# A hybrid decoder layer on one Trainium2 core: the weight sums of the output product's first pair, made ahead of time and kept in DRAM

## The chip, the cores and the metric

The kernel runs on one core of one Trainium2 chip. The core has TensorE (PE, matmuls), VectorE (DVE), ScalarE (ACT), GpSimd (POOL) and SyncE (SP), each with its own in-order queue of instructions, and 16 DMA engines for transfers. DMAs are issued here by SP and, in a few places, by ACT. The metric is the device time of the whole kernel in microseconds: the median of several runs.

## What is computed

One decoder layer on x of 512 tokens by 2048 features, all in float32:

```python
h = rms_norm(x, norm1_g)
proj = h @ w_in
qa, ka, va, ra, ga, qb, kb, vb = jnp.split(proj, split_points, axis=-1)
log_g = jax.nn.log_sigmoid(ga @ gla_gate_w2 + gla_gate_b) / GLA_GATE_TAU
out_a = gla_mixer(qa, ka, va, ra, log_g, gla_onorm_g)
out_b = dilated_mixer(rms_norm(qb), rms_norm(kb), vb, rel_bias)
mix = jnp.concatenate([out_a, out_b], axis=-1)
x = x + mix @ w_out
h2 = rms_norm(x, norm2_g)
x = x + (jax.nn.silu(h2 @ w_gate) * (h2 @ w_up)) @ w_down
```

out_a is a gated linear attention (4 heads, chunks of 64), out_b a dilated attention (8 heads) whose scores get a bias looked up in rel_bias. The product that the change is about is mix @ w_out, with w_out of 2048 by 2048.

## The kernel before

**Products in pairs.** The large products are computed a pair of column blocks at a time (class Pair). A pair takes two blocks w1, w2 of 512 columns of a weight and the 2048 contraction rows in four groups g of twice 256. For each group it holds four quarters of 256 rows by 512 columns (a and c from w1, b and d from w2; a and b from the group's first rows, c and d from its second), and multiplies by the Strassen-Winograd scheme: seven products P1, P5, P6, P3, P7, P2, P4 in place of eight. Three of them use a single quarter (SINGLE: P1 uses a, P3 uses d, P2 uses c). Four use a difference (SUMS_OF), made in place by VectorE at L256: P5 is b - a, written over a; P6 is d minus that, over a again; P7 is d - b, over b; P4 is c minus P6's sum, over a. The quarters are loaded by SP at L222 into tiles of 512 KB (wpool, 12 buffers).

**Items.** stream() runs over all pairs in order, over the seven products, over the four groups: 28 items a pair. For precision each item's weight is split: ACT casts it to wh (L331), VectorE subtracts to get wl (L335), and TensorE does 12 matmuls of 128x512 (L367), 8 with wh (against the high and low part of the activations) and 4 with wl. wh and wl have two buffers each, so the cast for item k+1 must wait until TensorE is done with item k-1. While item k is multiplied, the program gives the cast of k+1 (first_part), the sum of k+2 (total) and the subtraction for k+1 (second_part).

**The background.** After each item a pair's step function is called. It runs small pieces of other work (the attention chunks, the gates, the operands of the next product) from a list of generators, at a rate given pair by pair (rate, paced). Work tiles of 128x512 come from a pool with tag "r" and four buffers (rpool).

**Order.** The instructions of TensorE, VectorE and ACT are put in an order of their own by a scheduler that lists them for each engine (before the first stream by hand). DMAs are issued in program order on SP. Transfers are counted on eight semaphores, given in turn to those of SP and ACT, and each waits for the one before it on its own.

**The pairs.** After the first pair (qa, ka) come va; then qb and kb, first halves; then vb; then qb and kb, second halves; the gate; then two pairs of w_out (columns 0 to 1023 and 1024 to 2047), the up and gate products, and the down product. The change's words count the first pair as one: pairs two to four are va, qb0/kb0 and vb. A pair can have a before function that is called ahead of its first item. For the third pair (pairs[1]) it only lifts a hold on the order.

**The bias tables.** bias_tables() is a background job begun with the second pair. It makes the dilated attention's bias (bias_d, in DRAM) and at its end, L628, copies it from DRAM to DRAM, repeated for 128 partitions (rep_d, 2.5 MB). The dilated heads load from rep_d at L971.

Other lines that are spoken of: L566 copies a closed sum of a product out of PSUM with a scale (cout, ACT); L1109 stores such results (va, qb, kb, vb) on SP; L886 and its neighbours load q, k and v chunks back; L928 and L933 make the normed attention output oT, and L936 stores it as ong_d. L174 and L175 split activations of the output product in two (AA, AS); L1193 and L1237 load halves of mix from mix_d for them; L1251 to L1255 make their sums (r); L1129 turns the gated part of mix with matmuls into bank, from cr (L1178).

## Time and profile before

| | us |
|---|---|
| median of 3 runs | 1967.47 |
| lowest and highest | 1966.2, 1968.27 |
| the profiled execution, its own time | 1968.84 |
| its span | 1967.1 |

The profile was taken in a fourth execution. Its span runs from the first to the last instruction recorded; its own time also has what lies around it. A page gives busy times of the engines, the span in slices, the DMA queues, the chain of work that ended last, and groups of instructions: line, engine, operation, output <- inputs, count | busy us, mean ns of one | idle time of the engine just before them and what ended it. L is a line of the kernel before. PEld is the load of weights into TensorE, which overlaps its matmuls. A row of a timeline has start, duration, engine, line, operation, tiles, count, and in brackets the idle time ahead of it. ACTq and SPq are the issues of transfers on those queues. A row "A <- B: us, times, longest" sums the waits of A that B ended.

### The profile page before, as it was taken

How to read it: one execution, taken by the hardware profiler on the slowest of the kernel's cores; microseconds unless marked ns; L12 is line 12 of the kernel's file. 1: busy time of each engine (PE TensorE's matmuls, PEld its weight loads, DVE VectorE, ACT ScalarE, POOL GpSimd, SP SyncE). 2: the span in 40 equal slices, each digit the busy share in tenths (PEclk: the TensorE clock that was granted, in tenths of full speed). 3: DMA queues.
4: the chain of work that ended last, by engine and by line, in shares of the span. 5: the costliest groups of instructions: out<-in, count | busy, mean ns of one | idle time of the engine just before them, and what ended most of it. 6: DMA issues, size and time to landing. Idle time of an engine off the chain costs nothing.

```text
span 1967.1 us, 25785 instructions
## 1 busy us (share of the span) xinstructions
PE 1927.6 (98%) x9226; PEld 1670.9 (85%) x9226; DVE 1653.7 (84%) x1850; ACT 1093.8 (56%) x1600; POOL 60.9 (3%) x81
## 2 busy tenths in 40 slices
PE   8999999999999999999999999999999999999998
PEld 7888888888878877888888888888888888888887
DVE  8997787868789889878878878878879989989987
ACT  8554564566766766545545445545446646546443
POOL 0000230010000000000000000000000000000000
PEclk9999999999999999999999999999999999999999
DMA  8447455463766684554554553554555865855662
GB/s 278 141 162 266 119 171 170 134 200 124 221 213 202 215 288 152 177 167 133 178 170 127 179 163 127 176 164 130 172 163 168 299 203 185 310 183 175 236 214 75
DMA packets 237114, 360.45 MB, mean 183 GB/s; under 512 B 18246, under 2 KB 96783, under 8 KB 236984
## 3 DMA queue, kind: packets, MB, share of 16 engines
q1 hardware_dynamic: 236776, 358.72, 57.6%
q8 instruction: 72, 1.18, 0.3%
q14 instruction: 58, 0.48, 0.1%
q10 hardware_dynamic: 208, 0.08, 0.0%
HBM read 296.59 MB, written 64.51 MB: 184 GB/s over the span
## 4 chain that ended last, share of the span: by engine, by line
PE 75%; DVE 8%; DMA 5%; issue 3%; ACT 2%; POOL 0%; SPq 0%; DVEq 0%; ACTq 0%
PE acc L367 71%; DVE wl L335 3%; DVE wa L256 2%; PE bank L1129 1%; DVE AS L175 1%; PE bank L987 1%; DMA q<-in_x 1%; DMA xn_d<-oT 1%; ACT wh L331 1%; DMA q<-y_d 0%; DVE seed L294 0%; PE bank L1019 0%; DVE seed L1334 0%; DMA r<-xn_d 0%; DMA wc<-in_w_down 0%
## 5 line engine op out<-in xcount | busy, mean ns | idle before, releaser
L367 PE MATMUL acc<-wh,AS 128*128 128x512 f32 x3008 | 712.5, 380 | 0.6 <-ACT wh L331 0.5
L367 PEld LDWEIGHTS acc<-wh,AS 128*128 128x128 f32 x3008 | 569.8, 190 | 82.3 <-ACT wh L331 1.8
L331 ACT CAST wh<-wa 128x1024 fp32r<-128x1024 f32 x376 | 394.0, 1048 | 392.4 <-PE acc L367 363.0
L367 PE MATMUL acc<-wh,AA 128*128 128x512 f32 x2256 | 535.0, 380 | 0.0
L335 DVE TENSOR_TENSOR wl<-wa,wh 128x1024 fp32r<-128x1024 f32 x376 | 456.3, 1217 | 69.2 <-ACT wh L331 43.6
L367 PEld LDWEIGHTS acc<-wh,AA 128*128 128x128 f32 x2256 | 427.4, 190 | 61.4 <-ACT wh L331 0.9
L367 PE MATMUL acc<-wl,AS 128*128 128x512 f32 x1504 | 395.3, 385 | 9.7 <-DVE wl L335 9.5
L367 PEld LDWEIGHTS acc<-wl,AS 128*128 128x128 f32 x1504 | 279.4, 189 | 62.0 <-DVE wl L335 21.0
L367 PE MATMUL acc<-wl,AA 128*128 128x512 f32 x1128 | 298.1, 387 | 7.9 <-DVE wl L335 7.7
L367 PEld LDWEIGHTS acc<-wl,AA 128*128 128x128 f32 x1128 | 209.6, 190 | 41.5 <-DVE wl L335 12.4
L331 ACT CAST wh<-wb 128x1024 fp32r<-128x1024 f32 x94 | 98.5, 1049 | 129.7 <-PE acc L367 127.8
L331 ACT CAST wh<-wc 128x1024 fp32r<-128x1024 f32 x94 | 98.4, 1047 | 111.5 <-PE acc L367 101.7
L331 ACT CAST wh<-wd 128x1024 fp32r<-128x1024 f32 x94 | 98.5, 1048 | 105.8 <-PE acc L367 102.3
L256 DVE TENSOR_TENSOR wa<-wc,wa 128x1024 f32<-128x1024 f32 x94 | 114.4, 1221 | 46.2 <-DMA wc<-in_w_gate 25.1
L335 DVE TENSOR_TENSOR wl<-wc,wh 128x1024 fp32r<-128x1024 f32 x94 | 114.5, 1218 | 35.6 <-ACT wh L331 35.6
L335 DVE TENSOR_TENSOR wl<-wd,wh 128x1024 fp32r<-128x1024 f32 x94 | 114.3, 1219 | 34.9 <-ACT wh L331 28.2
L335 DVE TENSOR_TENSOR wl<-wb,wh 128x1024 fp32r<-128x1024 f32 x94 | 113.6, 1216 | 5.5 <-ACT wh L331 5.5
L256 DVE TENSOR_TENSOR wb<-wd,wb 128x1024 f32<-128x1024 f32 x94 | 114.3, 1216 | 1.1 <-DMA wd<-in_w_in 0.6
L256 DVE TENSOR_TENSOR wa<-wb,wa 128x1024 f32<-128x1024 f32 x94 | 113.6, 1218 | 0.8
L256 DVE TENSOR_TENSOR wa<-wd,wa 128x1024 f32<-128x1024 f32 x94 | 112.8, 1215 | 0.1
L298 DVE SCALAR_TENSOR_TENSOR seed<-acc,rs,seed 128x512 f32<-128x512 f32 x96 | 70.4, 745 | 24.9 <-PE acc L367 24.9
L282 ACT ACTIVATE seed<-acc,rs 128x512 f32<-128x512 f32 x96 | 60.6, 681 | 1.4 <-PE acc L367 0.8
(303 smaller groups left out, 1365.1 us busy)
## 6 DMA issues: line engine op xcount, KB each, us to landing
wa<-in_w_gate SPq DMA_DIRECT2D x44, 512.0 KB, 3.9
wb<-in_w_up SPq DMA_DIRECT2D x44, 512.0 KB, 4.3
wd<-in_w_up SPq DMA_DIRECT2D x44, 512.0 KB, 4.3
wc<-in_w_gate SPq DMA_DIRECT2D x44, 512.0 KB, 3.7
wc<-in_w_in SPq DMA_DIRECT2D x28, 512.0 KB, 3.9
wa<-in_w_in SPq DMA_DIRECT2D x24, 512.0 KB, 5.1
wb<-in_w_in SPq DMA_DIRECT2D x24, 512.0 KB, 6.0
wd<-in_w_in SPq DMA_DIRECT2D x24, 512.0 KB, 5.9
```

What stands on the lines that cost most here:

```text
L175: nc.vector.tensor_tensor(a[:, :, 1, :], src, a[:, :, 0, :].bitcast(F32), op=ALU.subtract)
L256: nc.vector.tensor_tensor(src, self.quarter(one, g), src, op=ALU.subtract)
L282: nc.scalar.activation(halves(t), unfolded(src[m]), AF.Copy, scale=self.scale(half, m))
L298: nc.vector.scalar_tensor_tensor(halves(seed[m]), unfolded(src[m]), self.scale(half, m), halves(seed[m]), op0=ALU.mult, op1=ALU.add,)
L331: nc.scalar.copy(high[k], sources[k])
L335: nc.vector.tensor_tensor(low[k], sources.pop(k), high[k].bitcast(F32), op=ALU.subtract)
L367: nc.tensor.matmul(p.dst[prod][m], a[:, jj, hl, m * P : (m + 1) * P], folded(w[:, jj, :]), start=fresh and g == 0 and len(terms) == 2 and ...
L987: nc.tensor.matmul(lp[:, :n], qh[:, b * P : (b + 1) * P], kh[:, :n], start=True, stop=True)
L1129: nc.tensor.transpose(bk[:, jj, m * P : (m + 1) * P], tiles[m][:, f : f + P], ident)
```

## The change

A new generator, weight_sums, makes the four differences of each group of the output product's first pair (w_out, columns 0 to 511 and 512 to 1023) while pairs two to four run, and stores them in 16 DRAM arrays (out_sums). It works in eight blocks of 128 rows (four groups, two halves). Block i starts 12 + 9i items after the second pair's first one; it fetches four pieces of 256 KB by DMAs issued on ACT (a and b at its start, d one item later, c two later) into the "r" tiles, subtracts them on VectorE four to seven items after its start, and stores each difference one item after it is made, again with DMAs issued on ACT. One item's worth is taken after each call of the pair's step function (beside). Every one of these instructions, 64 DMA issues and 32 subtractions of 128x512, is held in its place in program order by tc.keep_in_program_order; the scheduler orders the rest around it.

The output product's first pair is given sums=out_sums: source() then loads the ready difference, 512 KB, into a "w" tile (named ws) instead of computing it, and lets go of the single quarters after their one use. So it makes 28 loads of 512 KB (16 of them sums), in place of 16 loads, and none of its 16 sums at L256. 8 MB of w_out are fetched and 8 MB of sums stored in pairs two to four.

The copy of bias_d into rep_d is taken out of bias_tables (with one yield of that job) and put in the third pair's before function. In SP's order it comes a few loads later than it did. The instructions of GpSimd keep their order; those of the other engines shift.

```diff
--- before.py
+++ after.py
@@ -236,9 +236,10 @@
     class Pair:
 
 
-        def __init__(self, op, rows, w1, w2, final, step, scale=None, before=None):
+        def __init__(self, op, rows, w1, w2, final, step, scale=None, before=None, sums=None):
             self.op, self.rows, self.w1, self.w2 = op, rows, w1, w2
             self.final, self.step, self.scale, self.before = final, step, scale, before
+            self.sums = sums
             self.q, self.dst, self.held = {}, {}, {}
 
         def quarter(self, name, g):
@@ -250,7 +251,14 @@
         def source(self, prod, g):
 
             if prod in SINGLE:
-                return self.quarter(SINGLE[prod], g)
+                t = self.quarter(SINGLE[prod], g)
+                if self.sums:
+                    self.q.pop((SINGLE[prod], g))
+                return t
+            if self.sums:
+                t = wpool.tile([P, 2, 512], F32, name=nm("ws"), tag="w")
+                load(t, self.sums[prod, g])
+                return t
             one, two = SUMS_OF[prod]
             src = self.quarter(two, g)
             nc.vector.tensor_tensor(src, self.quarter(one, g), src, op=ALU.subtract)
@@ -314,6 +322,47 @@
             else:
                 which = {"P3": "P6", "P7": "P5", "P2": "P1"}[prod]
                 self.close(self.held[which], src, *CLOSES[prod])
+
+    def weight_sums(rows, w1, w2, sums):
+
+
+        tt, pinned = nc.vector.tensor_tensor, tc.keep_in_program_order
+        plan = {}
+
+        def at(group, fn):
+            plan.setdefault(group, []).append(fn)
+
+        def block(start, g, j):
+            t = {}
+
+            def fetch(name):
+                r0 = rows[g][0 if name in "ab" else 1] + P * j
+                t[name] = rpool.tile([P, 512], F32, name=nm("r"), tag="r")
+                pinned(nc.scalar.dma_start(t[name], (w1 if name in "ac" else w2)[r0 : r0 + P, :]))
+
+            def less(dst, one, two):
+                pinned(tt(t[dst], t[one], t[two], op=ALU.subtract))
+
+            def put(prod, name):
+                pinned(nc.scalar.dma_start(sums[prod, g][:, j, :], t[name]))
+
+            at(start, lambda: fetch("a"))
+            at(start, lambda: fetch("b"))
+            at(start + 1, lambda: fetch("d"))
+            at(start + 2, lambda: fetch("c"))
+            for i, (dst, one, two, prod) in enumerate(
+                (("a", "b", "a", "P5"), ("b", "d", "b", "P7"), ("d", "d", "a", "P6"),
+                 ("c", "c", "d", "P4"))
+            ):
+                at(start + 4 + i, lambda dst=dst, one=one, two=two: less(dst, one, two))
+                at(start + 5 + i, lambda prod=prod, dst=dst: put(prod, dst))
+
+        for i in range(8):
+            block(12 + 9 * i, i // 2, i % 2)
+        for n in range(max(plan) + 1):
+            for fn in plan.get(n, ()):
+                fn()
+            yield
 
     def stream(pairs):
 
@@ -536,6 +585,15 @@
             except StopIteration:
                 background.pop(0)
 
+    def beside(go, gen):
+
+
+        def both():
+            go()
+            next(gen, None)
+
+        return both
+
     def paced(counts):
         counts = iter(counts)
         return lambda: step(next(counts, 1))
@@ -625,8 +683,9 @@
             nc.vector.tensor_copy(lv, bp[:8, :cn])
             store(bias_d[:, c0 : c0 + cn], lv)
         yield
+
+    def repeat_bias():
         load(rep_d, bass.AP(tensor=bias_d.tensor, offset=0, ap=[[NB, 8], [0, P], [1, NB]]))
-        yield
 
     ss1 = const([P, 4, 4], "ss1")
     rs1 = const([P, 4], "rs1")
@@ -1297,16 +1356,23 @@
     def pair(*args, **kw):
         pairs.append(Pair(*args, **kw))
 
-    pair(opx, rows_in, col(1536), col(1024), final_proj("va1", "va0"), rate((22, 1), (6, 0.6)),
+    ocol = lambda c: w_out[:, c : c + 512]
+    rows_mix = [(1024 + 256 * g, 256 * order[g]) for g in range(4)]
+    out_sums = {
+        (prod, g): dram([P, 2, 512], f"{prod}_{g}_d") for prod in SUMS_OF for g in range(4)
+    }
+    early_sums = weight_sums(rows_mix, ocol(0), ocol(512), out_sums)
+    pair(opx, rows_in, col(1536), col(1024), final_proj("va1", "va0"),
+         beside(rate((22, 1), (6, 0.6)), early_sums),
          row_scale, before=lambda: background.extend([gates(), bias_tables()]))
     flow = rate((90, 0.41))
-    pair(opx, rows_in, col(3088), col(4112), final_proj("qb0", "kb0"), flow, row_scale)
-    pair(opx, rows_in, col(5648), col(5136), final_proj("vb1", "vb0"), flow, row_scale)
+    flowing = beside(flow, early_sums)
+    pair(opx, rows_in, col(3088), col(4112), final_proj("qb0", "kb0"), flowing, row_scale)
+    pair(opx, rows_in, col(5648), col(5136), final_proj("vb1", "vb0"), flowing, row_scale)
     pair(opx, rows_in, col(3600), col(4624), final_proj("qb1", "kb1"), flow, row_scale)
     pair(opx, rows_in, col(2048), col(2560), final_gate, rate((5, 0.6), (23, 1.05)), row_scale)
 
 
-    rows_mix = [(1024 + 256 * g, 256 * order[g]) for g in range(4)]
     x1_d = [dram([P, D], f"x1_d{t}") for t in range(4)]
     xn_d = [dram([P, 2, 512], f"xn_d{b}") for b in range(8)]
     ss2 = const([P, 4, 4], "ss2")
@@ -1417,7 +1483,6 @@
         turn()
         yield
 
-    ocol = lambda c: w_out[:, c : c + 512]
     def output_scales():
         tmp2 = const([P, 4], "tmp2")
         nc.vector.tensor_tensor(tmp2, ss2[:, :, 2], ss2[:, :, 3], op=ALU.add)
@@ -1430,7 +1495,7 @@
     opn = Operand(4)
     tops = [xn_d[2], xn_d[3], xn_d[6], xn_d[7]]
     bots = [xn_d[0], xn_d[1], xn_d[4], xn_d[5]]
-    pair(opm, rows_mix, ocol(0), ocol(512), final_out(0), paced([1] * 28))
+    pair(opm, rows_mix, ocol(0), ocol(512), final_out(0), paced([1] * 28), sums=out_sums)
     pair(opm, rows_mix, ocol(1024), ocol(1536), final_out(1), rate((28, 1.2)))
 
 
@@ -1568,7 +1633,7 @@
     behind = ExitStack()
     for engine in ("act", "dve", "pe"):
         behind.enter_context(tc.issue_after(recent[engine]))
-    pairs[1].before = behind.close
+    pairs[1].before = lambda: (behind.close(), repeat_bias())
     stream(pairs)
     drain()
```

## The prediction

> **What bounds the kernel now.** I read the busy shares first, then the chain's cost groups, and then the one stretch that the change wants to shorten, the output product's first pair.
>
> ```profile
> span 1967.1 us, 25785 instructions
> PE 1927.6 (98%) x9226; PEld 1670.9 (85%) x9226; DVE 1653.7 (84%) x1850; ACT 1093.8 (56%) x1600; POOL 60.9 (3%) x81
> L256 DVE TENSOR_TENSOR wa<-wb,wa 128x1024 f32<-128x1024 f32 x94 | 113.6, 1218 | 0.8
> L335 DVE TENSOR_TENSOR wl<-wa,wh 128x1024 fp32r<-128x1024 f32 x376 | 456.3, 1217 | 69.2 <-ACT wh L331 43.6
> ```
>
> TensorE is busy 98% of the span. All that any change to other engines can recover is where TensorE stands still. So the question is how much it stands still in the output product's first pair, and how much new standing still the early work makes. The L256 row prices one weight sum over a 512 KB quarter at 1.22 us of VectorE.
>
> The next fence has TensorE's order of time at both ends of that pair.
>
> ```profile
> 560.93 1.89 PE L367 MATMUL acc<-wh,AA 128*128 128x512 f32 x8
> ...
> 565.85 1.13 PE L367 MATMUL acc<-wl,AA 128*128 128x512 f32 x4 [0.43 <-DVE wl L335]
> ...
> 570.11 1.13 PE L367 MATMUL acc<-wl,AA 128*128 128x512 f32 x4 [1.40 <-DVE wl L335]
> 573.05 0.44 PE L1129 MATMUL bank<-mats,cr 128*128 128x128 f32 x2 [1.81 <-DVE cr L1178]
> ...
> 574.84 3.02 PE L367 MATMUL acc<-wh,AA 128*128 128x512 f32 x8
> ...
> 578.57 1.89 PE L367 MATMUL acc<-wh,AS 128*128 128x512 f32 x8
> ...
> 642.91 1.89 PE L367 MATMUL acc<-wh,AA 128*128 128x512 f32 x8
> ...
> 645.50 1.89 PE L367 MATMUL acc<-wh,AA 128*128 128x512 f32 x8
> ```
>
> An item (8 matmuls with wh, 4 with wl) takes 645.50 - 642.91 = 2.59 us when nothing holds TensorE. P1's four items run from 560.93 to 578.57, 17.6 us where 4 x 2.59 = 10.4 and 1.7 of turning (573.05 to 574.84) would do. The other 24 run from 578.57 to 645.50, 66.9 us where 24 x 2.59 = 62.2 would do: 4.8 us lost. Where, the windows say (columns: PE, PEld, DVE, ACT, POOL busy with counts, granted clock, DMA share, GB/s):
>
> ```profile
> 560.90:578.60 17.70, 13.89 (x58) 11.05 (x58) 17.38 (x22) 11.71 (x19) 0.00 (x0) 0.90 0.67 218
> 578.60:603.00 24.40, 21.25 (x93) 16.72 (x92) 23.49 (x29) 14.16 (x20) 0.00 (x0) 1.00 0.25 75
> 603.00:625.00 22.00, 22.00 (x104) 19.29 (x103) 22.00 (x27) 15.87 (x24) 0.00 (x0) 1.00 0.69 223
> ```
>
> From 603 us on TensorE is full, so the whole 4.8 us falls in 578.6 to 603, where VectorE is full and TensorE is not.
>
> **What the change takes away.** Sixteen L256 sums leave this pair. VectorE's order of time in the bound stretch, and at the start:
>
> ```profile
> 562.17 1.23 DVE L256 TENSOR_TENSOR wa<-wb,wa 128x1024 f32<-128x1024 f32 x1
> 563.43 1.23 DVE L256 TENSOR_TENSOR wb<-wd,wb 128x1024 f32<-128x1024 f32 x1
> ...
> 570.57 1.22 DVE L256 TENSOR_TENSOR wa<-wb,wa 128x1024 f32<-128x1024 f32 x1
> ...
> 580.11 1.22 DVE L256 TENSOR_TENSOR wa<-wb,wa 128x1024 f32<-128x1024 f32 x1
> 581.24 0.68 DVE L175 TENSOR_TENSOR AS<-r,AS 128x512 fp32r<-128x512 f32 x1
> 581.85 1.22 DVE L335 TENSOR_TENSOR wl<-wa,wh 128x1024 fp32r<-128x1024 f32 x1
> 582.98 0.68 DVE L1251 TENSOR_TENSOR r<-PT,r 128x512 f32<-128x512 f32 x1
> 583.58 1.22 DVE L256 TENSOR_TENSOR wa<-wb,wa 128x1024 f32<-128x1024 f32 x1
> ```
>
> One round of sum, AS, wl and r takes 583.58 - 580.11 = 3.47 us. Without the sum it is 583.58 - 581.24 = 2.34 us, below the item's 2.59. VectorE stops setting the pace there and the 4.8 us come back whole; that is my value for this part, and its lower bound is about 4, if AS waits once for its cast.
>
> At the start, two sums (2.4 us) stand ahead of the wl that TensorE misses at 565.85, and the one at 570.57 ahead of cr. But AA and AS there also hang on a load of mix_d, so only part comes forward. The waits give the ends: nothing, or 0.43 + 1.40 + 1.81 = 3.6 us. I take 2.0, since the 0.43 and some 0.9 of the 1.40 are the sums' and the later wait on cr shrinks by about 0.7. Gain 4.8 + 2.0 = 6.8, between 4 and 8.4.
>
> The matmul row at 574.84 took 3.02 us for what takes 1.89, right after TensorE's idle stretch, and the granted clock of its window is below 1. "TensorE: Matmul & The Clock Gate" of the Trainium skill (Part 1) says that the array's clock is cut after about 3.4 us of idleness; by that rule a shorter gap could also save this 1.1 us. It stays out of the sum.
>
> The pair's transfers grow: 16 loads of ready sums and 12 of single quarters take the place of 16, all of 512 KB, 14 MB for 8 MB. Over 84.6 us this adds 6 x 1.05 / 84.6 = 74 GB/s; the windows above show 218, 75 and 223 GB/s, with DMA shares of 0.67 and less. In SP's order these loads stand far ahead of their use. I cost them at nothing; without the cover a late quarter costs one landing, some 5 us.
>
> **What it adds in pairs two to four.** Eight blocks, each 4 fetches and 4 puts of 256 KB issued by ACT and 4 subtractions of 128x512. Rows of this size:
>
> ```profile
> 1.21 0.47 ACTq L584 DMA_DIRECT2D mats<-in_mats  x1
> ...
> L869 DVE TENSOR_TENSOR T<-k,oT 128x512 f32<-128x512 f32 x4 | 2.8, 689 | 4.2 <-ACT oT L862 4.2
> ...
> 120.00:360.00 240.00, 237.19 (x1164) 203.49 (x1164) 186.38 (x219) 124.73 (x220) 36.54 (x43) 1.00 0.58 183
> 320.00:360.00 40.00, 40.00 (x195) 35.25 (x194) 26.82 (x34) 18.25 (x27) 1.77 (x4) 1.00 0.86 269
> ...
> PE acc L367 <- DVE wl L335: 2.8, 5, 0.9
> ```
>
> The blocks lie within about 133 to 360 us. VectorE gets 32 x 0.69 = 22 us and has 240 - 186.4 = 53.6 us free in the first window; ACT gets 64 x 0.47 = 30 us of issuing and has 115 us free. TensorE loses only 2.8 us to wl between 108 and 400 us (the last row, a sum of waits). By amount everything is covered. A single stolen slot is covered by the two wh and wl buffers: the cast has almost 2.4 us of slack per item. So a subtraction costs something only where it meets a full VectorE. For all 32 I take 0.5 us; the ends are 0 and 0.69 x 8 = 5.5, one late wl per block.
>
> What amounts do not show is **who is queued behind whom**. An ACT issue that has to wait, for a subtraction or for an earlier DMA on its completion lane (the program gives SP's and ACT's transfers eight semaphores in turn, and each waits for the one before it on its own), holds the casts behind it; and SP waits for lanes that ACT's transfers hold, or for the four r buffers. In the new order the sharpest place is the boundary of pairs two and three:
>
> ```profile
> 178.50 1.05 ACT L331 CAST wh<-wa 128x1024 fp32r<-128x1024 f32 x1 [3.63 <-PE acc L367]
> ...
> 183.47 1.26 ACT L566 ACTIVATE cout<-acc,rs 128x512 f32<-128x512 f32 x2 [0.24 <-PE acc L367]
> ...
> 197.69 1.05 ACT L331 CAST wh<-wa 128x1024 fp32r<-128x1024 f32 x1 [0.58 <-DVE wl L335]
> ```
>
> ```profile
> 172.82 1.70 SPq L222 DMA_DIRECT2D wb<-in_w_in  x2
> ...
> 183.48 1.89 PE L367 MATMUL acc<-wh,AA 128*128 128x512 f32 x8
> ...
> 202.97 1.89 PE L367 MATMUL acc<-wh,AS 128*128 128x512 f32 x8
> ...
> SPq L1109 <- ACT cout L566: 5.8, 1, 5.8
> ...
> wb<-in_w_in SPq DMA_DIRECT2D x24, 512.0 KB, 6.0
> ```
>
> The cast of pair three's first item ran at 178.50, 5 us before its use at 183.48. It now stands behind the two cout copies, which need the end of P4. With some attention matmuls moved behind P4, P4 ends near 181.9 and cout near 183.0; the cast ends near 184.1, so TensorE waits 0.6 us, or up to 1.5 if less of that filler is there. I take 1.0.
>
> Second, SP's loads of wb for P5 went out at 172.82; now they stand behind the cout stores, on which SP already waited 5.8 us, behind the ong_d stores, and behind v<-va, which waits for a fetch that ACT issues only after a cast near 191. I put the third wb at about 196.5. With 6.0 us to land, 1.22 for the sum and 1.05 for the cast, wh is ready near 204.8, where the same wh was used at 202.97 (cast at 197.69), now some 1 us later: 0.8 us of waiting, between 0 and 2.5. The other boundaries have nothing so tight in the order, but the same kind of queue; for them and ACT's lane waits I take 0.7, between 0 and 4.
>
> The copy of the bias tables moves by a few places of SP's order:
>
> ```profile
> L628 SPq DMA_DIRECT2D rep_d<-bias_d x1: 718/718/718, 141.2 to 141.2; - x1
> ...
> L971 SPq DMA_DIRECT2D T<-rep_d x4: 338/418/454, 327.2 to 497.9; - x4
> ```
>
> Its first reader is at 327, so that the copy itself costs nothing. It shares a lane with one fetch of block two, near 170, which is after its landing; without that margin ACT would stand still behind it, which is in the 4 us above.
>
> "DMA: Bandwidth & Descriptors" of the Trainium skill (Issuing engines are not separate DMA queues) speaks against the choice of ACT's queue: transfers issued from several engines share the same 16 DMA engines, and only issuing time is saved. By it the 16.8 MB of fetches and puts compete with the pairs' own loads, worst where the 320 to 360 row already has a share of 0.86; no row here shows ACT and SP transfers competing at that point.
>
> **Sum.** -6.8 + 0.5 + 1.0 + 0.8 + 0.7 = -3.8 us. Against the profiled execution, 1968.84 us, this is 1965.0; that execution lies 1.4 us above the median 1967.47 of the runs shown, so on the median the forecast is **1963.7 us**. With the gain between 4 and 8.4 and losses between 0.6 and 6, the case's own range is 1959.7 to 1969.5.
>
> **Rivals.**
>
> *ACT becomes the new wait (slower).* ACT is in order; a put that waits on a lane or a fetch holds the next cast. The nearest row is where ACT waits for a store today:
>
> ```profile
> ACT oT L928 <- DMA ong_d<-oT: 1.9, 2, 1.2
> ```
>
> At 1.2 us twice per block (once at a fetch, once at a put) beyond what the cast's slack covers, eight blocks cost 19 us; minus the 6.8 this is +12, or 1980. At once per block it is 9.6 - 6.8 = +2.8, 1970. It decides against the change from 0.85 us per block on. For it: 64 issues, each with a wait on its lane's predecessor, and SP has a history of waiting on late producers. Against it: most predecessors landed tens of microseconds before, and the slack is 2.4 us per item. I take 1975 for this case, chance 0.26.
>
> *The output product is not freed (about the same).* If mix_d's load and the chain to cr hold the start whatever VectorE does, and the casts of AS hold the middle, 3 us come back, and 3 are lost: 1967.5. For it: AA waits for mix_d. Against it: the 3.47 us round is plainly VectorE's own. Chance 0.18.
>
> *Full relief.* Everything that P1 loses and the clock's dip come back: 17.64 - 10.4 - 1.7 = 5.5 with the 4.8, minus a loss of 1: -9.3, or 1958. The early work then costs nothing but the boundary. Chance 0.14.
>
> **How the numbers follow.** My forecast has 0.42. A measurement of this kernel can tell 0.2% from no change, about 3.9 us, so faster begins below 1963.5. The forecast's case gives 0.24 to faster and 0.18 to same; full relief 0.14 to faster; the unfreed product 0.17 to same and 0.01 to slower; ACT's case 0.25 to slower and 0.01 to same. Faster 0.38, same 0.36, slower 0.26. The range for 8 in 10 goes from 1957, where full relief ends, to 1976, which holds half of ACT's case.
>
> **What would show each step.** In the changed profile: the 578 to 603 stretch at 2.59 us per item with no L256 group on wa<-wb between 560 and 620; the waits of TensorE on wl there below 1 us together (right), or the same 3.5 us rounds (wrong). TensorE's wait at the boundary near 184 and in P5 near 204; idle time of TensorE from 120 to 360, now 240 - 237.2 = 2.8 us, at about 6. In ACT's waits between 130 and 360, a DMA as releaser with more than 10 us in total and the same idleness on TensorE would mean that the first rival holds. The forecast is wrong if TensorE's added idle time before 360 exceeds what 560 to 646 gives back.

## The result, and the profile after

The change makes the kernel 0.2% slower: 1971.68 us median of 14 runs (1966.85 to 1979.36) against 1967.71 us of 14 runs of the kernel before, ratio 1.0021 with a 95% interval of 1.0011 to 1.003. The forecast was 1963.7 us. Runs of the new kernel also scatter about three times as widely in this comparison (12.5 us against 3.7). Lines named from here on are those of the changed kernel where its profile is shown: L380 is the cast to wh (L331 before), L384 the subtraction to wl (L335), L416 the matmul (L367), L264 the sum (L256). P_d stands for the stored sums, so P_d<-r is an early put and r<-in_w_out an early fetch.

First the page of the kernel after, busy times and queues (q10 is the queue of ACT's transfers):

```profile
span 1970.7 us, 25922 instructions
PE 1929.7 (98%) x9226; PEld 1673.4 (85%) x9226; DVE 1654.2 (84%) x1866; ACT 1094.0 (56%) x1600; POOL 53.6 (3%) x81
...
q1 hardware_dynamic: 237992, 365.01, 57.8%
q10 hardware_dynamic: 9424, 16.86, 2.5%
...
L416 PE MATMUL acc<-wh,AS 128*128 128x512 f32 x3008 | 714.3, 381 | 5.8 <-ACT wh L380 5.8
```

VectorE's total is the same (the sums moved, they did not go), 16.86 MB of traffic are new, and a wait of TensorE is there that was not: 5.8 us on casts. To place it, the table below lines up the two profiles by item. TensorE's matmuls were counted off in twelves; for each item it gives how much later its first matmul starts than in the profile of before, less the difference at item 0. Items 0 to 27 are the pair va, 28 to 55 qb0/kb0, 56 to 83 vb, 84 to 139 the next two, 140 to 167 the output product's first pair, 168 to 195 its second. All later tables have the same columns.

| start of item | 28 | 36 | 48 | 84 | 140 | 168 | 224 |
|---|---|---|---|---|---|---|---|
| after, us late | 0.8 | 8.0 | 11.9 | 14.3 | 13.3 | 7.7 | 3.3 |

So 14.3 us are lost by item 84, where the early work ends; 5.6 come back in the output product's first pair (13.3 to 7.7), and another 5.4 in places that the change does not touch (14.3 to 13.3, and 7.7 to 3.3). Two steps stand out in the loss, 32 to 36 and 44 to 48.

TensorE's waits in the kernel after, from 100 to 400 us, and its order of time at the two steps:

```profile
PE acc L416 <- DVE wl L384: 6.6, 7, 2.0
PE acc L416 <- ACT wh L380: 5.8, 3, 4.1
```

```profile
209.41 3.62 PE L416 MATMUL acc<-wh,AS 128*128 128x512 f32 x8 [4.05 <-ACT wh L380]
...
249.91 1.75 PE L416 MATMUL acc<-wl,AS 128*128 128x512 f32 x4 [1.98 <-DVE wl L384]
251.45 3.01 PE L416 MATMUL acc<-wh,AS 128*128 128x512 f32 x8
```

Against 2.8 us before, TensorE waits 12.4 us. Each step also pays twice: after its wait, eight matmuls take 3.62 and 3.01 us in place of 1.89. The first wait leads back through ACT and VectorE to a load. ACT's order of time, then VectorE's:

```profile
208.31 1.04 ACT L380 CAST wh<-wa 128x1024 fp32r<-128x1024 f32 x1 [6.70 <-DVE wa L264]
```

```profile
206.97 2.48 DVE L264 TENSOR_TENSOR wa<-wb,wa 128x1024 f32<-128x1024 f32 x2 [5.95 <-DMA wb<-in_w_in]
...
244.14 1.23 DVE L264 TENSOR_TENSOR wa<-wc,wa 128x1024 f32<-128x1024 f32 x1 [2.12 <-DMA wc<-in_w_in]
```

VectorE waits 6 us for the third wb of the third pair, and ahead of the second step for wc: weight loads, which SP issues. SP's order of time in the kernel after, and what SP itself waited for from 190 to 200 us:

```profile
173.03 1.63 SPq L222 DMA_DIRECT2D wa<-in_w_in  x3
182.72 0.92 SPq L1168 DMA_DIRECT2D va<-cout  x2
...
187.98 0.80 SPq L995 DMA_DIRECT2D ong_d<-oT  x2
188.83 1.00 SPq L222 DMA_DIRECT2D wb<-in_w_in  x2
...
193.54 0.89 SPq L995 DMA_DIRECT2D ong_d<-oT  x2
194.48 3.14 SPq L897 DMA_DIRECT2D T<-ls_d  x3
...
199.01 0.51 SPq L904 DMA_DIRECT2D v<-va  x1
199.56 0.98 SPq L222 DMA_DIRECT2D wb<-in_w_in  x2
200.84 4.08 SPq L222 DMA_DIRECT2D wd<-in_w_in  x4
```

```profile
SPq L995 <- DVE oT L992: 2.8, 1, 2.8
SPq L897 <- DMA P_d<-r: 1.7, 2, 1.2
```

The third wb goes out at 199.56 where it went out at 172.82 before. It stands behind stores that wait for the attention, and behind the loads T<-ls_d, which wait until early puts have landed, since they share a semaphore with them. Then it shares the DMA engines with the fourth wb, four wd and the block's own transfers. A windows row of the kernel before and one of the kernel after, the columns as in the prediction:

```profile
190.00:210.00 20.00, 19.80 (x95) 16.73 (x94) 19.14 (x19) 10.92 (x14) 6.26 (x3) 1.00 0.21 62
```

```profile
190.00:210.00 20.00, 14.92 (x68) 11.84 (x67) 11.04 (x12) 6.83 (x12) 0.99 (x3) 0.98 0.96 309
```

Before, these 20 us were a lull for the DMA engines (share 0.21, 62 GB/s), since the pair's weights were already there. After, they are full (0.96, 309 GB/s). Not all of that is the early work's, as the run with the copy moved alone shows below.

In the output product's first pair the change does what it says. Its waits of TensorE, 574 to 660 us, and a window where the sums stood before:

```profile
PE acc L416 <- DVE wl L384: 1.6, 1, 1.6
PE acc L416 <- ACT wh L380: 0.8, 1, 0.8
PE bank L1188 <- DVE cr L1237: 0.8, 1, 0.8
```

```profile
590.10:610.80 20.70, 20.70 (x97) 18.15 (x96) 20.39 (x27) 17.13 (x27) 0.00 (x0) 1.00 0.99 347
```

P5 and P6 now run without a gap: TensorE is busy 20.70 of 20.70 us, 8 items at 2.59. The row shows full DMA engines too, 0.99 and 347 GB/s, with the ready sums among the loads.

### The profile page after: what moved, and what is told of

Its sections match the earlier page's. It is cut to its first block, busy times and chain, and to the rows that moved or that the text cites. A ratio compares the mean times of both kernels' runs of the same rounds, so it can differ in the third digit from the quotient of the medians.

```text
span 1970.7 us, 25922 instructions
## 1 busy us (share of the span) xinstructions
PE 1929.7 (98%) x9226; PEld 1673.4 (85%) x9226; DVE 1654.2 (84%) x1866; ACT 1094.0 (56%) x1600; POOL 53.6 (3%) x81
## 3 DMA queue, kind: packets, MB, share of 16 engines
q10 hardware_dynamic: 9424, 16.86, 2.5%
## 4 chain that ended last, share of the span: by engine, by line
PE 57%; DVE 5%; DMA 3%; issue 2%; ACT 1%; SPq 0%; DVEq 0%; ACTq 0%
PE acc L416 56%; DVE wl L384 2%; PE bank L1188 1%; DVE wa L264 1%; DVE AS L175 1%; DMA wc<-in_w_down 1%; DMA wb<-in_w_down 0%; DMA xn_d<-oT 0%; DVE seed L1400 0%; DMA r<-xn_d 0%; DVE seed L302 0%; DMA wd<-in_w_down 0%; DMA xn_d<-PT 0%; DVE AA L175 0%; DMA k<-y_d 0%
## 5 line engine op out<-in xcount | busy, mean ns | idle before, releaser
L416 PE MATMUL acc<-wh,AS 128*128 128x512 f32 x3008 | 714.3, 381 | 5.8 <-ACT wh L380 5.8
L416 PEld LDWEIGHTS acc<-wh,AS 128*128 128x128 f32 x3008 | 570.8, 190 | 88.5 <-ACT wh L380 7.8
L380 ACT CAST wh<-wa 128x1024 fp32r<-128x1024 f32 x364 | 381.4, 1049 | 385.8 <-PE acc L416 346.8
L416 PE MATMUL acc<-wh,AA 128*128 128x512 f32 x2256 | 534.3, 380 | 1.5 <-ACT wh L380 1.4
L384 DVE TENSOR_TENSOR wl<-wa,wh 128x1024 fp32r<-128x1024 f32 x364 | 442.1, 1218 | 63.9 <-ACT wh L380 39.3
L416 PEld LDWEIGHTS acc<-wh,AA 128*128 128x128 f32 x2256 | 427.1, 190 | 62.5 <-ACT wh L380 2.4
L416 PE MATMUL acc<-wl,AS 128*128 128x512 f32 x1504 | 395.7, 386 | 9.0 <-DVE wl L384 8.8
L416 PEld LDWEIGHTS acc<-wl,AS 128*128 128x128 f32 x1504 | 280.0, 189 | 60.5 <-DVE wl L384 19.7
L416 PE MATMUL acc<-wl,AA 128*128 128x512 f32 x1128 | 297.6, 386 | 7.6 <-DVE wl L384 7.5
L416 PEld LDWEIGHTS acc<-wl,AA 128*128 128x128 f32 x1128 | 209.5, 189 | 41.4 <-DVE wl L384 11.9
L380 ACT CAST wh<-wb 128x1024 fp32r<-128x1024 f32 x90 | 94.2, 1048 | 127.5 <-PE acc L416 115.9
L380 ACT CAST wh<-wc 128x1024 fp32r<-128x1024 f32 x94 | 98.4, 1047 | 118.7 <-PE acc L416 107.1
L380 ACT CAST wh<-wd 128x1024 fp32r<-128x1024 f32 x94 | 98.4, 1048 | 102.7 <-PE acc L416 99.8
L384 DVE TENSOR_TENSOR wl<-wc,wh 128x1024 fp32r<-128x1024 f32 x94 | 114.6, 1220 | 40.7 <-ACT wh L380 40.6
L264 DVE TENSOR_TENSOR wa<-wc,wa 128x1024 f32<-128x1024 f32 x90 | 109.8, 1222 | 46.1 <-DMA wc<-in_w_gate 23.9
L384 DVE TENSOR_TENSOR wl<-wd,wh 128x1024 fp32r<-128x1024 f32 x94 | 114.4, 1220 | 33.7 <-ACT wh L380 26.8
L264 DVE TENSOR_TENSOR wa<-wb,wa 128x1024 f32<-128x1024 f32 x90 | 108.6, 1219 | 7.1 <-DMA wb<-in_w_in 6.4
L384 DVE TENSOR_TENSOR wl<-wb,wh 128x1024 fp32r<-128x1024 f32 x90 | 108.8, 1217 | 3.3 <-ACT wh L380 3.3
L264 DVE TENSOR_TENSOR wb<-wd,wb 128x1024 f32<-128x1024 f32 x90 | 109.4, 1217 | 0.4
L264 DVE TENSOR_TENSOR wa<-wd,wa 128x1024 f32<-128x1024 f32 x90 | 108.1, 1216 | 0.1
```

Of the source, the lines that this page charges most:

```text
L264: nc.vector.tensor_tensor(src, self.quarter(one, g), src, op=ALU.subtract)
L380: nc.scalar.copy(high[k], sources[k])
L384: nc.vector.tensor_tensor(low[k], sources.pop(k), high[k].bitcast(F32), op=ALU.subtract)
L416: nc.tensor.matmul(p.dst[prod][m], a[:, jj, hl, m * P : (m + 1) * P], folded(w[:, jj, :]), start=fresh and g == 0 and len(terms) == 2 and ...
```

## The experiments

Each kernel was run beside the kernel before on the same chip. The lateness figures of the expectations are without the correction at item 0; the tables have it (0.1 to 1.6 us per profile). They come from one profile each, and the runs of most of these kernels scatter by some microseconds, so differences below about 2 us are not read. Some profiled executions lie well off their kernel's median (without subtractions 3.6 us above it, GpSimd's queue 2.4 below, the kernel before 1.4 above), so the medians are read beside them. The ratio is the recorded one and not the quotient of the two medians.

**The two halves by themselves.** First the early work alone:

```diff
-    pair(opm, rows_mix, ocol(0), ocol(512), final_out(0), paced([1] * 28), sums=out_sums)
+    pair(opm, rows_mix, ocol(0), ocol(512), final_out(0), paced([1] * 28))
```

> The early sums are made and stored as in the change, but the output product's first pair makes its own sums again, as before; nothing is left out of the result. In the changed profile TensorE is 14.4 us late by the start of the fifth pair (item 84: 373.44 us against 358.99) and then wins about 10 us back. Theory Q (queues: the loss comes from the early work alone, by the order and the waits of SP's and ACT's transfers): item 84 is again 12 to 16 us late and nothing is won back, so the median is 12 to 16 us above before, near 1982. Rival U (the lost time belongs to the two parts together, or is noise of one profile): item 84 less than 7 us late, median below 1975.

Then the use alone, in which the ready sums are plain quarters of w_out and no early work is done:

```diff
-        (prod, g): dram([P, 2, 512], f"{prod}_{g}_d") for prod in SUMS_OF for g in range(4)
+        (prod, g): ocol(0)[256 * g : 256 * g + 256, :].rearrange("(j p) n -> p j n", p=P)
+        for prod in SUMS_OF for g in range(4)
...
-    early_sums = weight_sums(rows_mix, ocol(0), ocol(512), out_sums)
+    early_sums = iter(())
...
-    pairs[1].before = lambda: (behind.close(), repeat_bias())
+    pairs[1].before = behind.close
```

> The output product's first pair loads its sums ready made, but they are never made: in their place it loads plain quarters of w_out, so the output's values differ; no early work, and the copy of the bias tables stands where it stood. This is the gain alone. By the prediction's term 6.8 us are gained (4 to 8.4), median near 1961; by the changed profile, where lateness falls from 13.44 at item 140 to 3.44 at item 224, it is up to 10 us, median near 1957.5. Rival (the gain seen there was only slack that a late start gives back): 3 us or less, median 1964.5 or more.

And the copy's move alone, on the kernel before:

```diff
-        load(rep_d, bass.AP(tensor=bias_d.tensor, offset=0, ap=[[NB, 8], [0, P], [1, NB]]))
-        yield
+    def repeat_bias():
+        load(rep_d, bass.AP(tensor=bias_d.tensor, offset=0, ap=[[NB, 8], [0, P], [1, NB]]))
...
-    pairs[1].before = behind.close
+    pairs[1].before = lambda: (behind.close(), repeat_bias())
```

> The kernel before with one edit: the copy of the bias tables is taken out of its job and put in the third pair's before function. By the prediction's term it costs nothing: within 1.5 us of before. Rival: the copy's place changes the order of the background's loads at the boundary near 180 us by itself, 3 us or more slower, and item 36 is late.

| kernel | median us | ratio to before (95%) | 28 | 36 | 48 | 84 | 140 | 168 | 224 |
|---|---|---|---|---|---|---|---|---|---|
| early work alone | 1977.43 | 1.006 (1.0044 to 1.0076) | 0.7 | 7.8 | 12.0 | 13.9 | 13.0 | 12.6 | 9.7 |
| use alone | 1961.04 | 0.9975 (0.9958 to 0.9991) | 0.0 | -0.4 | -0.4 | -0.4 | -0.7 | -4.7 | -6.3 |
| copy moved alone | 1967.86 | 1.0005 (0.9995 to 1.0014) | -0.2 | 1.0 | 3.0 | 3.1 | 2.2 | 1.3 | -1.6 |

The two halves add up: 1977.43 and 1961.04 are +10.6 and -5.8 against the 1966.83 of before beside them, together +4.8, and the change measured +4.0. The gain was forecast at 6.8 and is 5.8. Of the gain, items 144 to 152 (P5 and P6) bring 4.7 in the use alone and 4.8 in the change, as forecast; P1 brings 0.6 and 1.9 of the 2.0 forecast. The loss is 13.9 us where it is made and 9.7 by item 224. The expectation had the median at 12 to 16 above before, and it came to 10.6. It is not shown why some 4 us come back: the use alone, which is not late, also wins 1.6 from item 168 to 224.

The copy's move costs 3.1 us by item 84 in its profile, though over the whole kernel its interval includes no change (+1.0 us), so the price of nothing held for the total. SP's order of time in that kernel, with no early work in it, then VectorE's:

```profile
172.62 1.52 SPq L222 DMA_DIRECT2D wa<-in_w_in  x3
182.31 0.92 SPq L1110 DMA_DIRECT2D va<-cout  x2
...
195.28 0.98 SPq L222 DMA_DIRECT2D wb<-in_w_in  x2
```

```profile
202.15 2.49 DVE L256 TENSOR_TENSOR wa<-wb,wa 128x1024 f32<-128x1024 f32 x2 [4.17 <-DMA wb<-in_w_in]
```

This is the order of the change already: wa behind the va stores, the third wb at 195.28 (172.82 before). Moving one 2.5 MB copy by a few places has put the third pair's loads behind stores that wait for the attention's results. By itself that costs 1.0 us at item 36. VectorE has the wb 6.9 us after its issue here, against 7.4 in the change, and the DMA engines are as full without any early work: share 0.96, 318 GB/s from 195 to 207 us, where the change has 0.97 and 317. So the landing under a full load comes with the order alone; what the early work adds is that the load goes out 4.3 us later, 199.56 for 195.28.

**Which cause in the early work.** Four runs undo one thing each. The transfers on GpSimd's queue:

```diff
-                pinned(nc.scalar.dma_start(t[name], (w1 if name in "ac" else w2)[r0 : r0 + P, :]))
+                pinned(nc.gpsimd.dma_start(t[name], (w1 if name in "ac" else w2)[r0 : r0 + P, :]))
...
-                pinned(nc.scalar.dma_start(sums[prod, g][:, j, :], t[name]))
+                pinned(nc.gpsimd.dma_start(sums[prod, g][:, j, :], t[name]))
```

> The whole change, with its 64 fetches and puts issued by GpSimd's queue in place of ACT's, held in order there; no other edit. Theory Q says that ACT no longer stands behind lanes and SP no longer waits for the puts' semaphores: item 84 at most 5 us late (14.4 in the change) and the median 1960 to 1965, below before. Rival B (bandwidth: 16.8 MB compete with the weight loads whichever queue issues them): item 84 again 10 us or more late, median 1968 to 1974. Rival D (VectorE's 32 subtractions are what costs): the same as B.

The copy back where it stood (the inverse of the diff of the copy's move):

> The whole change, but with the copy of the bias tables left at the end of its job, where it stood before; SP's third and fourth wb of the third pair then stand ahead of the cout and ong_d stores again, as in the kernel before. Theory O (order: most of the early loss comes from the copy's new place, which moves the third pair's weight loads behind those stores): item 36 at most 3 us late (8.17 in the change, 1.72 with the copy's move alone), item 84 at most 7, and with the gain the median near 1962 to 1965. Rival T (traffic: the 16.8 MB and 64 issues themselves make those loads late, wherever they stand): item 36 at least 6 us late and item 84 at least 11, median 1969 to 1972.

No subtractions:

```diff
-                at(start + 4 + i, lambda dst=dst, one=one, two=two: less(dst, one, two))
+                pass
```

> The whole change, copy moved too, but without its 32 subtractions on VectorE: the pieces fetched are stored as they are, so that the output's values differ; all 64 transfers stay. Theories O and T: VectorE's amount is not the cost, so item 36 is 6 to 8 us late and item 84 9 to 13 (14.4 in the change), median 1967 to 1970. Rival D (the subtractions, through a full VectorE or as what ACT's puts wait for): item 84 at most 6 us late, median 1963 or less.

Nothing held in program order:

```diff
-        tt, pinned = nc.vector.tensor_tensor, tc.keep_in_program_order
+        tt, pinned = nc.vector.tensor_tensor, lambda i: i
```

> The whole change without holding the 64 issues and 32 subtractions in program order; the scheduler places them. Theory O: in SP's order the third pair's wb loads stand ahead of the cout stores here although the copy is moved, so item 36 is at most 3 us late; ACT's own queue may lose or gain some, item 84 3 to 9 us late, median 1961 to 1968. Rival T: item 36 at least 6 us late, median 1969 or more.

And the copy one pair later:

```diff
-    pairs[1].before = lambda: (behind.close(), repeat_bias())
+    pairs[1].before = behind.close
+    pairs[2].before = repeat_bias
```

> The whole change with the copy of the bias tables in the fourth pair's before function in place of the third's. By SP's order all eight wa and wb loads of the third pair then stand ahead of the later va stores, earlier than in the kernel before. Theory O: item 36 at most 3 us late, median 1962 to 1966; the copy, nearer its first reader, costs nothing as long as it lands before. Rival T: item 36 at least 6 us late, median 1969 to 1972.

| kernel | median us | ratio to before (95%) | 28 | 36 | 48 | 84 | 140 | 168 | 224 |
|---|---|---|---|---|---|---|---|---|---|
| GpSimd's queue | 1970.24 | 1.0021 (1.0011 to 1.003) | 0.0 | 6.6 | 7.4 | 10.6 | 8.8 | 3.1 | -1.4 |
| copy back | 1971.66 | 1.0018 (1.0009 to 1.0028) | 5.7 | 8.1 | 8.8 | 11.4 | 10.9 | 3.8 | 1.0 |
| no subtractions | 1970.23 | 1.0011 (1.0001 to 1.0021) | 0.7 | 9.4 | 10.9 | 12.3 | 10.7 | 4.6 | 1.8 |
| nothing held | 2017.95 | 1.025 (1.023 to 1.0271) | 56.1 | 57.0 | 57.0 | 57.0 | 55.3 | 48.1 | 44.8 |
| copy in the fourth pair | 1973.8 | 1.0028 (1.0015 to 1.0041) | 0.9 | 9.2 | 9.8 | 11.8 | 11.0 | 5.4 | 2.0 |

The expectation that the order made by the copy is by itself most of the loss (O) fell: with the copy back item 36 is as late as ever (8.1), although the wb loads stand ahead of the cout stores again. The stall has moved. SP's order of time in that kernel (its line numbers are one less in places), and what its stores waited for from 148 to 165 us:

```profile
150.39 12.08 SPq L1167 DMA_DIRECT2D va<-seed  x2
162.57 0.39 SPq L222 DMA_DIRECT2D wc<-in_w_in  x1
...
177.91 0.93 SPq L222 DMA_DIRECT2D wb<-in_w_in  x2
```

```profile
SPq L1167 <- DMA rep_d<-bias_d: 11.4, 1, 11.4
```

ACT's order of time and VectorE's there, and the same wc load in the kernel before:

```profile
168.31 1.04 ACT L380 CAST wh<-wc 128x1024 fp32r<-128x1024 f32 x1 [6.79 <-DMA va<-seed]
```

```profile
168.23 1.23 DVE L264 TENSOR_TENSOR wa<-wc,wa 128x1024 f32<-128x1024 f32 x1 [5.46 <-DMA wc<-in_w_in]
```

```profile
149.91 0.43 SPq L222 DMA_DIRECT2D wc<-in_w_in  x1
```

A cast of the second pair waits 6.8 us. The profile names the landing of a va store, which comes at nearly the same moment, but the cast reads wc, and VectorE's row shows that this wc has just landed. SP sent it out at 162.57, where it went out at 149.91 before, because the second va store ahead of it stood 11.4 us until the 2.5 MB copy, on the same semaphore, had landed. ACT's transfers take their turns on the eight semaphores, so the store now meets the copy's. So ACT is kept waiting, but through SP, and not by transfers of its own as the first rival has it. Without holding the order it gets far worse; what SP and ACT waited for:

```profile
SPq L1168 <- DMA r<-in_w_out: 70.9, 3, 69.4
```

```profile
ACT wh L380 <- DMA va<-seed: 41.9, 1, 41.9
```

There one va store of SP stands 69.4 us for the landing of an early fetch on its semaphore. The wc load behind it goes out at 215.61, VectorE has it at 220.71, and the cast, after 41.9 us of ACT's idleness, starts at 220.76.

GpSimd's queue, where ACT is free of the transfers, still leaves 10.6, so ACT's own waits are not the main cost when the copy is moved, and theory Q (at most 5) fell. The subtractions are not most of it either (12.3 without, 14.3 with); the profile is of an execution 3.6 us above its median, and by the medians they can be worth up to some 2 of the 4 us. The copy in the fourth pair tells nothing new: the order came out as in the change and not as the expectation assumed, with the third wb issued at 199.62 us, and so did the stall.

**Both suspects at once, and the bytes.** The copy back and GpSimd's queue together:

> The whole change with both suspects undone: the copy of the bias tables stands where it stood, and the 64 transfers are issued by GpSimd's queue in place of ACT's, so that no cast stands behind a transfer's wait; all traffic and all subtractions stay. With the copy back alone, item 36 was 9.0 us late and item 84 12.4, the stall having moved to item 24, where ACT waited for the landing of a va store; with GpSimd's queue alone, 7.0 and 11.0. Theory L+O (two causes, each enough to make the stall: ACT's casts behind waits for the semaphores that SP's transfers hold, and the third pair's weight loads behind stores): item 36 at most 3 us late, item 84 at most 6, median 1961 to 1965. Rival T (the traffic itself makes the loads late): item 36 at least 6, item 84 at least 10, median 1968 to 1971.

The early work alone, 64 columns wide (transfers and subtractions), an eighth of the bytes:

```diff
-                t[name] = rpool.tile([P, 512], F32, name=nm("r"), tag="r")
-                pinned(nc.scalar.dma_start(t[name], (w1 if name in "ac" else w2)[r0 : r0 + P, :]))
+                t[name] = rpool.tile([P, 512], F32, name=nm("r"), tag="r")[:, :64]
+                pinned(nc.scalar.dma_start(t[name], (w1 if name in "ac" else w2)[r0 : r0 + P, :64]))
...
-                pinned(nc.scalar.dma_start(sums[prod, g][:, j, :], t[name]))
+                pinned(nc.scalar.dma_start(sums[prod, g][:, j, :64], t[name]))
```

> As the run in which the sums are made but not used, with the same 64 issues and 32 subtractions in the same order, but each only 64 columns wide in place of 512 (32 KB in place of 256), so an eighth of the traffic; the sums stored are incomplete and nothing reads them. Item 84 was 14.8 us late there. Theory L+O: order and waits stay, transfers land a little sooner, so item 84 is 8 to 13 us late. Rival T: item 84 at most 5 us late.

The same with the copy back:

> The run with 64-column transfers, again with sums that nothing reads, but with the copy of the bias tables where it stood: ACT's queue, all 64 issues and their waits, an eighth of the bytes. Against the full width with the copy back, where item 84 was 12.4 us late. If waits and order cost by themselves (theory W), item 84 stays 5 us late or more. If the bytes do it, by making every landing late on which ACT and SP wait (theory T), item 84 is at most 1.5 us late.

And with the copy back, full fetches and subtractions, and only the puts 64 columns wide:

> The same with the fetches and subtractions at full width and only the puts cut to 64 columns (8.4 MB fetched, 1 MB stored); nothing reads the sums. Theory T: the loss follows the bytes whichever way they go, item 84 between the 1/8 width and the full width, 3 to 8 us late. Theory W: 5 us or more, as in the 1/8 width. A third way, that the puts alone do it (ACT waits on landings of puts): at most 2 us late.

| kernel | median us | ratio to before (95%) | 28 | 36 | 48 | 84 | 140 | 168 | 224 |
|---|---|---|---|---|---|---|---|---|---|
| copy back, GpSimd's queue | 1963.66 | 0.9985 (0.9976 to 0.9995) | 0.6 | 4.3 | 4.9 | 7.1 | 5.3 | -0.6 | -3.6 |
| sums unused, 64 wide | 1970.02 | 1.002 (1.001 to 1.0031) | -0.2 | 3.9 | 4.1 | 2.8 | 1.7 | 3.0 | 0.3 |
| sums unused, 64 wide, copy back | 1967.9 | 1.0009 (0.9997 to 1.002) | 1.3 | 2.7 | 2.7 | 2.3 | 0.7 | 1.2 | -0.7 |
| sums unused, puts 64 wide, copy back | 1977.0 | 1.0044 (1.0015 to 1.0073) | 2.6 | 5.1 | 6.5 | 9.5 | 7.4 | 8.2 | 6.5 |

Undoing both suspects gives a kernel faster than before, with the median that was expected for two causes (1961 to 1965), though 7.1 us are still lost by item 84 (at most 6 were expected). By the medians, if the gain stays at 5.8, the change loses 9.8 us, the copy back alone 9.1, GpSimd's queue alone 9.2, and both together 2.5. So either arrangement by itself is enough for most of the loss.

The width is needed too. All 64 issues in the same places, an eighth as wide, cost 2.8 us by item 84 in place of 13.9 (copy moved), and 2.3 in place of 11.4 (copy back). With the copy moved, SP's order of time shows why:

```profile
195.67 0.99 SPq L222 DMA_DIRECT2D wb<-in_w_in  x2
```

The third wb goes out 3.9 us sooner than at full width, and VectorE has it at 202.83, 7.2 us later. So the bytes act less on the landing of this load (7.4 in the change) than on its issue, through the landings for which SP waits. With the copy back SP still stands 10.1 us for the copy, but wc goes out at 160.49, 2.1 us sooner, which takes away most of the wait. Theory T holds in so far as the bytes are needed; its bounds were missed (2.3 against 1.5 in the narrow run with the copy back, 9.5 against 3 to 8 with narrow puts). The loss comes with the full fetches and subtractions (2.3 to 9.5); the bytes of the puts, 1.9 more, are below what is read here. The narrow runs shrink the subtractions too; what share of the 7.2 is VectorE's when the copy is back was not separated. In that arrangement VectorE does count somewhere: with copy back and GpSimd's queue, the one wait above 2 us is on wl, in a stretch where VectorE has an early subtraction (L344), the pair's own sums (L264) and wl in a row (TensorE's, then VectorE's order of time):

```profile
195.11 2.03 PE L416 MATMUL acc<-wl,AA 128*128 128x512 f32 x4 [2.21 <-DVE wl L384]
```

```profile
189.33 0.68 DVE L344 TENSOR_TENSOR r<-r,r 128x512 f32<-128x512 f32 x1
189.94 1.22 DVE L264 TENSOR_TENSOR wa<-wb,wa 128x1024 f32<-128x1024 f32 x1
191.19 1.24 DVE L264 TENSOR_TENSOR wb<-wd,wb 128x1024 f32<-128x1024 f32 x1
193.04 0.88 DVE L991 SCALAR_TENSOR_TENSOR oT<-bank,so,gb 128x256 f32<-128x256 f32 x2 [0.62 <-POOL so L159]
193.84 2.35 DVE L384 TENSOR_TENSOR wl<-wa,wh 128x1024 fp32r<-128x1024 f32 x2
```

**Less early work.** VectorE sets the pace of the output product in P5 and P6 only; from 603 us on TensorE was full in the kernel before, with the later sums in place. So the last version makes only the sums of P5 and P6 early, keeping the copy back and GpSimd's queue (on top of the diffs above):

```diff
             if prod in SINGLE:
-                t = self.quarter(SINGLE[prod], g)
-                if self.sums:
-                    self.q.pop((SINGLE[prod], g))
-                return t
-            if self.sums:
+                return self.quarter(SINGLE[prod], g)
+            if self.sums and prod in ("P5", "P6"):
                 t = wpool.tile([P, 2, 512], F32, name=nm("ws"), tag="w")
                 load(t, self.sums[prod, g])
+                self.q["a", g] = t
                 return t
...
-            at(start + 2, lambda: fetch("c"))
...
-                (("a", "b", "a", "P5"), ("b", "d", "b", "P7"), ("d", "d", "a", "P6"),
-                 ("c", "c", "d", "P4"))
+                (("a", "b", "a", "P5"), ("d", "d", "a", "P6"))
```

> Only the sums of P5 and P6 are made early, those of P7 and P4 where they were (24 fetches, 16 puts and 16 subtractions; 10.5 MB in place of 16.8); transfers on GpSimd's queue, the copy where it stood. By the stretch 578 to 603, where VectorE sets the pace, P5 and P6 bring nearly the whole gain: items 140 to 152 again 5 to 6 us faster. Theory L+O: item 84 at most 5 us late, median 1961 to 1965. Rival T: the loss follows the bytes, item 84 6 to 8 us late, median 1966 to 1968.

And with ACT's queue:

> The same with the transfers on ACT's queue, as in the change, the copy where it stood. Theory L+O: ACT's casts stand again behind waits for SP's transfers, item 84 6 to 12 us late and the median 2 to 6 us above the one on GpSimd's queue. Rival T: within 1.5 us of the one on GpSimd's queue.

| kernel | median us | ratio to before (95%) | 28 | 36 | 48 | 84 | 140 | 168 | 224 |
|---|---|---|---|---|---|---|---|---|---|
| two sums, GpSimd's queue | 1958.17 | 0.9957 (0.994 to 0.9974) | 0.6 | 1.2 | 1.7 | 1.2 | -0.4 | -8.2 | -11.5 |
| two sums, ACT's queue | 1960.29 | 0.997 (0.9959 to 0.9982) | 1.4 | 3.4 | 3.9 | 2.8 | 0.9 | -6.1 | -9.8 |

Both beat the kernel before and the change. With 10.5 MB, 40 issues and 16 subtractions in place of 16.8 MB, 64 and 32, the early loss is 1.2 us, and the output product gains 7.8 (items 140 to 168). Windows of the version on GpSimd's queue in that pair:

```profile
560.00:576.00 16.00, 13.64 (x68) 10.99 (x67) 13.65 (x19) 12.44 (x21) 0.00 (x0) 1.00 0.96 313
576.00:600.00 24.00, 24.00 (x113) 21.02 (x112) 24.00 (x31) 20.90 (x32) 0.00 (x0) 1.00 0.79 267
600.00:620.00 20.00, 20.00 (x94) 17.50 (x94) 20.00 (x23) 9.59 (x13) 0.00 (x0) 1.00 0.75 238
```

TensorE is full from 576 on, although VectorE makes the sums of P7 there and is full as well. On GpSimd's queue the early loss is within what theory L+O expected (at most 5), and the median below both forecasts; on ACT's queue it is 2.8 us where 6 to 12 were expected. The two versions' intervals overlap, so that GpSimd's queue is the better of the two here is not shown.

## Why the prediction was wrong, point by point

*What bounds the kernel, and the gain.* Right. The 3.47 us rounds were VectorE's, P5 and P6 run at 2.59 now, and L264 is gone from that stretch. The term 6.8 measured 5.8 by the use alone and 5.6 in the change. The 4.8 of P5 and P6 came (4.7 and 4.8), the 2.0 of P1 came in the change (1.9) and not in the use alone (0.6), and about 1 us is lost again at P3, where TensorE waits 0.8 us for a cast. The second rival (the product not freed) and the third (full relief) are out.

*Amounts on VectorE and ACT.* Right for what they claim, as far as one profile tells: without the subtractions the loss is still 12.3 of 14.3. By amount the early work was covered.

*The boundary of pairs two and three.* The first part, the cast behind cout, cost nothing by itself (item 28 is 0.8 late, and 1.0 of lateness was there at item 20). The second, the third wb of P5, was the right place with the wrong size: priced at 0.8 us between 0 and 2.5, it took 5.6 (items 32 to 36). This term is **the step that failed** first. By its sum wh would be ready near 204.8; it was ready at 209.35, 4.5 us later. Of these, 3.1 are the issue, estimated at 196.5 and made at 199.56, and 1.4 the landing, taken as 6.0 us from a row of before and 7.4 here (199.56 to 206.97). The issue would have been about right without the early work's bytes: 195.28 with the copy moved alone, 195.67 with narrow transfers. At full width SP's stores wait longer for the attention and its loads T<-ls_d wait for the early puts' landings; how the 4 us divide between these was not separated. The longer landing hardly needs the early work: it is 6.9 with the copy moved alone, where wb and wd go out together too. What followed was also left out: the low clock after a 4 us wait, 3.62 us for eight matmuls in place of 1.89.

*The other boundaries and ACT's lane waits, 0.7 us between 0 and 4.* This term failed with it. They took the rest: 14.3 by item 84, less 5.6 and less 1.6 around items 28 to 32, is 7.1. The largest is 3.9 at items 44 to 48 behind a late wc; the copy's move alone has 2.0 of lateness there (1.0 to 3.0). The prediction named the kind of queue, SP waiting for semaphores that ACT's transfers hold, and then said that nothing was as tight; in the copy-back run one such wait is 11.4 us.

*The copy of the bias tables, priced at nothing.* Right by itself and over the whole kernel (+1.0 us, an interval that includes no change), though its profile is 3.1 us late at item 84. Its first reader had indeed time enough. What was missed is how the move and the early work act together. And where the copy stays in its place, its landing on a semaphore shared with SP's stores, which the prediction looked for on ACT only, is what stops SP.

*The bytes.* The Trainium skill's rule on the page "DMA: Bandwidth & Descriptors" (Issuing engines are not separate DMA queues), that transfers of several issuing engines share the same DMA engines, was set against the change in the prediction and left out of the sum. These runs agree with it: GpSimd's queue alone, with the same bytes, still costs 10.6 us by item 84, and an eighth of the bytes on ACT's queue 2.8. What the queue changes besides is on whose semaphores SP waits: with the copy back, 11.4 us for the copy's landing with ACT's queue and none with GpSimd's. The worst place was 190 to 210 us and not, as feared, 320 to 360.

*The forecast as a whole.* It had 3.0 us of loss against 6.8 of gain; the loss is 9.8 on the medians, with the gain at 5.8. The ends of its four loss terms, 5.5, 1.5, 2.5 and 4, add up to 13.5, and its range took 6 without a reason. The first rival, ACT as the new wait, came closest: 1975 was its price, 1971.7 was measured, and the loss of 9.8 is near its 9.6 for one wait per block. Its test is met: releases of ACT by DMAs add up to 14.6 us from 130 to 360 (5.4, 4.2, 3.8 and smaller), and TensorE's idle time from 120 to 360 rose from 2.8 to 12.4. Even so the nearness is in part luck, since its mechanism is not the larger one: ACT's waits are few and long and not one or two per block, the largest stall comes through SP's loads, and without ACT's queue most of the loss stays.

The loss by item 84, in us (one profile each; in the 64-wide runs nothing reads the sums):

| | copy moved | copy back |
|---|---|---|
| ACT's queue, full width | 14.3 | 11.4 |
| GpSimd's queue, full width | 10.6 | 7.1 |
| ACT's queue, 64 wide | 2.8 | 2.3 |
| no early work | 3.1 | 0 |

In these profiles full width is worth 9 to 11.5 us, the queue 4, the copy's place 3. On the medians the queue alone and the copy's place alone are worth less than 1 us each and the two together 7, so the causes work together and these differences are not prices to be added. Open are the share of the fetches' bytes against the full-width subtractions with the copy back, and which of fewer bytes, issues or subtractions makes the two-sum version so much cheaper.

## What to carry to other kernels

Ask of every load in the new order when its queue will be free to issue it: the wb load here went out 27 us later and took 1.4 us longer to land than reckoned. Where transfers of two engines share completion semaphores in turn, new transfers on one queue can make the other stand until a slow copy has landed. Before moving work out of a bound stretch, take only the part that sets the pace there: two of four sums, with the copy back, brought the whole gain for a small part of the loss.

## What the runs showed of the hardware

The granted clock can fall after a wait of about 2 us. TensorE stood still 1.98 us before 249.91, and the windows after it (columns as before) show it at 0.57 of the full clock for 4 us (0.50 from 250.3 to 253.7):

```profile
248.00:250.00 2.00, 0.09 (x1) 0.09 (x1) 2.00 (x4) 1.94 (x7) 0.00 (x0) 1.00 0.26 87
250.00:252.00 2.00, 2.00 (x6) 1.62 (x7) 2.00 (x3) 1.42 (x4) 1.34 (x2) 0.57 0.59 146
252.00:254.00 2.00, 2.00 (x7) 1.61 (x6) 2.00 (x4) 1.10 (x6) 0.74 (x1) 0.57 0.96 237
254.00:256.00 2.00, 2.00 (x11) 1.76 (x10) 1.62 (x3) 1.45 (x5) 0.07 (x1) 1.00 1.00 316
```

"TensorE: Matmul & The Clock Gate" of the Trainium skill (Part 1) puts the drop after an idle window of about 3.4 us. Here it came after 1.98 us, so the measurement decides: the step from item 44 to 48 costs 3.9 us, of which only 1.98 are the wait, and nearly all the rest is slow matmuls (3.01 us for eight in place of 1.89, among others). The length of the wait does not settle it: with the copy back the clock fell to 0.50 after a wait of 2.53 us that ended at 169.41, and stayed at 1.00 after one of 2.52 that ended at 201.51.
